# Attention scores of a hybrid decoder layer: hi and lo parts packed as two halves of 64 rows, and mask with row maximum in one vector instruction

## The chip, the core and the metric

The kernel runs on one core of one Trainium2 chip. The metric is the device time of one execution in microseconds (us). Several executions were timed; the median is used, and a profile was taken of one further execution.

## The reference

The layer takes 1024 tokens of width 1024 in float32. A normalised input is projected once, and the columns of that projection feed two mixers side by side: a Mamba-2 scan (SSD, 16 heads of 64) and differential attention (8 heads). Their outputs are joined, projected, and a gated feed-forward network (FFN) and a last norm follow. The change concerns the differential attention:

```python
q = q.reshape(bsz, seqlen, DA_HEADS, 2, DA_HEAD_DIM).transpose(3, 0, 2, 1, 4) * (DA_HEAD_DIM ** -0.5)
k = k.reshape(bsz, seqlen, DA_HEADS, 2, DA_HEAD_DIM).transpose(3, 0, 2, 1, 4)
...
        s = jnp.einsum("mbhqd,mbhkd->mbhqk", qi, k).astype(f32)
        qpos = i * Q_BLOCK + jnp.arange(Q_BLOCK)
        mask = kpos[None, :] <= qpos[:, None]
        p = jax.nn.softmax(jnp.where(mask, s, -jnp.inf), axis=-1)
        w = p[0] - lam * p[1]
        return jnp.einsum("bhqk,bhkv->bhqv", w.astype(v.dtype), v)
```

Every head has two maps (m = 0 and 1). Each map has its own 64 columns of q and k, its own causal softmax, and the difference of the two maps weights v. A block is 128 queries, so a head has 8 blocks, and block i sees (i + 1) x 128 keys.

## The kernel before

The work stands in the program in this order: the mixer norm; the SSD part in two groups; the attention, head by head; the output projection (lines 660 to 725); the FFN; the down projection. All arithmetic of the matmuls is of float32 accuracy: an operand is split into a rounded part "hi" (type `float32r`) and the exact rest "lo", and a product is taken as hi·hi + hi·lo + lo·hi. `mm3` (lines 126 to 129) is that product, three matmuls into one accumulator; the projections, the output projection and the FFN all use it.

The order on each engine is not written out by hand in the attention. The tile framework orders the instructions of the whole program by its own simulated time line, within the dependencies and with the pools as limits. So projections of the next heads stand between the attention matmuls of the present one. From line 909 on, TensorE's order is the written one.

One head of the attention runs through these functions.

- `v_pair` (line 527) projects v for two heads. `qk` (line 543) projects k and q for one head: `proj_T` gives 128 columns (64 of each map) by 512 tokens in a PSUM tile, for two halves of the tokens, and a sink takes it out of PSUM.
- `sink_k` (lines 547 to 553) writes a tile `KS` with one plane for each map: k-hi of the map on its own 64 rows and k-lo of the same map on the other 64 rows. That is one ScalarE copy and one VectorE subtraction of 64x512 for each map.
- `sink_q` (lines 555 to 566) writes `QH` and `QL`, again a plane for each map, with q-hi (or q-lo) on both halves of the rows. For each map that is a ScalarE multiplication (562), a VectorE instruction (563), and a copy to the other half on ScalarE (565) and on VectorE (566).
- `att_front` (lines 572 to 598) makes the scores of one block. With that packing, one matmul over all 128 rows gives q-hi·(k-hi + k-lo), a second gives q-lo·(k-hi + k-lo): lines 585 and 586, for each map and each chunk of at most 512 keys. Block i has one chunk for i below 4 and two from there on. Then VectorE adds the causal mask `cneg` to the 128 columns of the diagonal (587), takes the negated row maximum (588), and ScalarE takes the exponential with the row sum (590). Lines 593 to 597 join the two maps.
- `att_back` (line 600) transposes the weights (607), copies them out (608) and multiplies by v (611). `att_norm` and `att_out` follow later. `step` calls them one block or more behind the front.

Score tiles come from the pool `SC`, which has two buffers of 1024 columns (two banks of PSUM each). `KS`, `QH` and `QL` come from `A4`, 14 buffers of 1024 float32 columns; for the last head one tile of `QL` comes from `CV`. The exponentials are in `P4`. The output projection's first part (line 696, tiles `po_s`) needs the SSD output alone and runs beside the last heads; its loads of x and its stores of h are issued from GpSimd's queue (695 and 698), as are the loads of h (704).

Of the kernel before, what the change touches and what calls it, by code (L numbers as in the profile page):

```python
# [9 lines left out]
F32 = mybir.dt.float32  # L10
F32R = mybir.dt.float32r
AF = mybir.ActivationFunctionType
ALU = mybir.AluOpType
# [11 lines left out]
def tile_hybrid_block(  # L25
# [68 lines left out]
    def norm_rows(parts, wbc, outs, name, pool=(), junk=None):  # L94
        """outs = RMSNorm of the row whose column pieces are parts; pieces in pool are weighted on Pool and scaled on ACT"""
        n, w = len(parts), DM // len(parts)
        ss = small.tile([P, n], F32, tag="ss1", name="ss_" + name)
        for i, p in enumerate(parts):
            nc.scalar.activation(outs[i] if junk is None else junk, p, AF.Square, accum_out=ss[:, i:i + 1])
        if n > 1:  # L100
            s1 = small.tile([P, 1], F32, tag="ss1", name="st_" + name)
            nc.vector.tensor_tensor(s1, ss[:, 0:1], ss[:, 1:2], op=ALU.add)
            ss = s1
        r = rstd_of(ss, DM, name)
        for i, (p, o) in enumerate(zip(parts, outs)):
            wi = wbc[:, i * w:i * w + w]
            if i in pool:
                nc.gpsimd.tensor_tensor(o, p, wi, op=ALU.mult)
                nc.scalar.mul(o, o, r)
            else:  # L110
                nc.vector.scalar_tensor_tensor(o, p, r, wi, op0=ALU.mult, op1=ALU.mult)
# [34 lines left out]
    def A4(shape, dt, name):  # L146
        return a4.tile(shape, dt, tag="a4", name=name)
# [15 lines left out]

# [1 line left out]
    def load_raw(src, shape, name):  # L165
# [14 lines left out]
    def z0_raw(a, u):  # L180
        """columns of dt and of the gate of group 0: 264 of 528"""
        raw = wp.tile([P, 4, 264], F32, tag="raw", bufs=2, name=f"wr_z0_{a}_{u}")
        k = slice(4 * u, 4 * u + 4)
        if a == 0:
            nc.sync.dma_start(raw[:, :, 0:16], w_in_k[:, k, C_DT:C_DT + 16])
            nc.sync.dma_start(raw[:, :, 16:264], w_in_k[:, k, C_Z:C_Z + 248])
        else:
            nc.sync.dma_start(raw, w_in_k[:, k, C_Z + 248:C_Z + 512])
        return raw
# [6 lines left out]

# [1 line left out]
    xs = []  # L198
# [16 lines left out]

# [1 line left out]
    prow = P4([69, P], F32, "prow")  # L217
# [17 lines left out]

# [1 line left out]
    def w_unit(src, shape, name, alloc=None):  # L237
# [10 lines left out]
    def proj_T(*jobs):  # L248
        """each job: a weight, a column, a name and sink(half, psum [128 columns, 512 tokens])"""
        us = [w_unit(w_k[:, :, col:col + P], [P, KD, P], name) for w_k, col, name, _ in jobs]  # L250
# [7 lines left out]
    def proj_z0(us, name, sink):  # L258
        """units of 264 columns; sink(t, psum [128 tokens, 264])"""
        for t in range(NT):  # L260
# [8 lines left out]
    def proj_nat(col, name, sink):  # L269
        """256 columns; sink(t, psum [128 tokens, 2 blocks from t, 256])"""  # L270
        us = [w_unit(w_in_k[:, 4 * u:4 * u + 4, col:col + 256], [P, 4, 256], f"{name}_{u}") for u in range(2)]
# [9 lines left out]

# [1 line left out]
    W16 = [P, NT, 16]  # L283
# [49 lines left out]

# [1 line left out]
    def conv_tiles(*tiles):  # L335
# [21 lines left out]
    def gate_dt():  # L357
        """the gate of group 0 and dt"""
        for a in range(2):
# [151 lines left out]

# [1 line left out]
    cneg = sp.tile([P, P], F32, tag="cs", name="cneg")  # L513
    nc.vector.memset(cneg, 0.0)
    nc.gpsimd.affine_select(cneg, cneg, [[-1, P]], ALU.is_ge, NEG, base=0, channel_multiplier=1)
    lv = CV([P, 4, 64], F32, "lv")
# [10 lines left out]
    def v_pair(hh):  # L527
        # [head][block] views of the two heads; in the last pair but one, the heads' tiles are freed one by one
        by_head = hh == NH // 2 - 2
# [13 lines left out]
    def qk(h):  # L543
        KS, QH, QL = [], [], []
        own = (slice(0, 64), slice(64, 128))

        def sink_k(half, ps):
            ks = A4([P, 2, 512], F32R, f"KS{h}_{half}")
            KS.append(ks)
            for m in range(2):  # L550
                a, b = own[m], own[1 - m]
                nc.scalar.copy(ks[a, m, :], ps[a, :])
                nc.vector.tensor_tensor(ks[b, m, :], ps[a, :], ks[a, m, :].bitcast(F32), op=ALU.subtract)

        def sink_q(half, ps):
            qh = A4([P, 2, 512], F32R, f"QH{h}_{half}")
            ql = (CV if h == NH - 1 and half == 0 else A4)([P, 2, 512], F32R, f"QL{h}_{half}")
            QH.append(qh)
            QL.append(ql)
            for m in range(2):  # L560
                a, b = own[m], own[1 - m]
                nc.scalar.mul(qh[a, m, :], ps[a, :], 0.125)
                nc.vector.scalar_tensor_tensor(ql[a, m, :], ps[a, :], 0.125, qh[a, m, :].bitcast(F32),
                                               op0=ALU.mult, op1=ALU.subtract)
                nc.scalar.copy(qh[b, m, :], qh[a, m, :].bitcast(F32))
                nc.vector.tensor_copy(ql[b, m, :], ql[a, m, :].bitcast(F32))
        jobs = ((w_in_k, C_K + h * P, f"k{h}", sink_k), (w_in_k, C_Q + h * P, f"q{h}", sink_q))
        for js in ([jobs] if h == NH - 1 else [[j] for j in jobs]):
            proj_T(*js)
        return KS, QH, QL  # L570

    def att_front(h, i, KS, QH, QL):
        n = f"{h}_{i}"
        Lk = (i + 1) * P
        qs = slice(i * P, (i + 1) * P)
        pm = []
        nmx = small.tile([P, 2], F32, tag="nmx", name="nmx" + n)
        sm = small.tile([P, 2], F32, tag="sm", name="sm" + n)
        for m in range(2):
            s = SC([P, T], f"s{n}_{m}")  # L580
            qr = slice((i % 4) * P, (i % 4) * P + P)
            for c in range(i // 4 + 1):
                w = min(Lk - c * 512, 512)
                sc = s[:, c * 512:c * 512 + w]
                nc.tensor.matmul(sc, QH[i // 4][:, m, qr], KS[c][:, m, :w], start=True, stop=False)
                nc.tensor.matmul(sc, QL[i // 4][:, m, qr], KS[c][:, m, :w], start=False, stop=True)
            nc.vector.tensor_tensor(s[:, qs], s[:, qs], cneg, op=ALU.add)
            nc.vector.reduce_max(nmx[:, m:m + 1], s[:, :Lk], axis=AX.X, negate=True)  # L588
            p = P4([P, T], F32, f"p{n}_{m}")
            nc.scalar.activation(p[:, :Lk], s[:, :Lk], AF.Exp, bias=nmx[:, m:m + 1], accum_out=sm[:, m:m + 1])  # L590
            pm.append(p)
# [67 lines left out]

# [1 line left out]
    KG = 4  # L661
# [14 lines left out]
    def out_block(t, kys, ws, name, bank=MM):  # L676
        """two token blocks from t, 256 columns"""
        ps = bank([P, 2, 256], f"po_{name}_{t}")
# [47 lines left out]

# [1 line left out]
    # gate and up by Winograd's seven products: A are two column tiles by two halves of the contraction, B the two  # L728
    # halves of the contraction by two halves of the tokens; C = A B is summed up in PSUM (X, Y and Z)
    ORDER = (1, 2, 6, 5, 7, 3, 4)  # L730
# [4 lines left out]
    def room(p, early):  # L735
        """an operand B: [hi or lo][block of 128 rows] views of 512 tokens"""
        if early:
# [59 lines left out]
    def ffn_pair(pr, raws, order=ALL, ybank=SC):  # L797
        """silu(gate) * up of two column tiles; they and their sums as operands of the down projection to g_d"""
        sg, tm, c22, reg, sm = {}, {}, {}, [{}, {}], [{}, {}]
# [145 lines left out]
    def final_half(t, nh, last):  # L945
        """the first half of a row to be ready is weighted before its scale is known"""
        ho = h_parts(ho_all, t)
# [12 lines left out]

    # down, by the same seven products: A are the two halves of the tokens by two row tiles, B the row tiles by two
    # halves of the columns
    SLOT = {2: 0, 4: 1, 1: 2, 7: 3, 5: 4, 6: 5, 3: 6}
# [28 lines left out]
    for gi, prs in enumerate(groups):  # L992
# [5 lines left out]
        def psums(two, name):  # L998
            """four banks: one for each block of 128 tokens of a half"""
            if two:  # L1000
# [81 lines left out]
```

## Time and profile before

| | us |
|---|---|
| median of 3 runs | 1641.82 |
| lowest, highest | 1639.54, 1644.53 |
| span of the profiled execution | 1643.3 |

The profile is read as follows. "PE" is TensorE's matmuls and "PEld" its weight loads; DVE is VectorE, ACT ScalarE, POOL GpSimd. Busy time is the time in which at least one instruction of the engine is recorded. A matmul is recorded from its start to a modelled end, and the next one starts before that end; so the distance from one start to the next, its pitch, says how fast the stream runs, and the recorded duration does not. The shape `128*128 128x512` names the stationary operand and then the moving one, so 512 is the number of keys or tokens that one matmul streams. The attention's first score matmul starts at 387 us and its last at 848 us; projections of the heads start somewhat earlier, beside the SSD scan.

| stretch of the span, us | what runs in it | PE busy | DVE busy | ACT busy |
|---|---|---|---|---|
| 0 to 340 | norm, SSD | 320.11 | 187.39 | 184.62 |
| 340 to 860 | end of SSD, attention, first output projection | 514.13 | 378.03 | 304.46 |
| 860 to 1643 | output projection, FFN, down | 763.00 | 506.17 | 286.76 |

### The profile page before, as it was taken

To read this page: it belongs to the slowest core of one execution; us is meant where nothing else is said; L and a number is where in the kernel's file an instruction comes from. 1 tells how busy PE (TensorE), PEld (TensorE's weight loads), DVE (VectorE), ACT (ScalarE), POOL (GpSimd) and SP (SyncE) were. 2 spreads that over 40 slices of the span, in tenths; PEclk is the share of its full clock that TensorE was granted. 3 is DMA by queue.
4 is the path that set the end of the run, shared out by engine and by line. 5 is a ranking of instruction groups with operands and counts; after the bars stand their busy time and mean duration, and the time that the engine had idled before them with its cause. 6 is when DMAs were issued, how large, how long until landed. Compare 5 with 4: busy or idle time off the path is not lost. (4 is left out here: it accounts for less than half of the span.)

```text
span 1643.3 us, 23716 instructions
## 1 busy us (share of the span) xinstructions
PE 1597.2 (97%) x9170; PEld 1386.9 (84%) x9170; DVE 1071.6 (65%) x1682; ACT 775.8 (47%) x1608; POOL 429.2 (26%) x378
## 2 busy tenths in 40 slices
PE   6999999999999999999999998999999999999997
PEld 6988878887989989889999987888888888778885
DVE  5345745688776676677674477455555555898987
ACT  6444764456555565575552245333333333334445
POOL 4100330032000000013300034444444443542322
PEclk9999999999999999999999999999999999999999
DMA  5321451143011110147523221233333323944122
GB/s 195 110 79 52 129 163 56 36 142 92 24 46 39 46 33 27 45 130 229 162 77 116 84 99 56 96 102 104 111 116 118 98 96 134 365 166 186 39 103 103
DMA packets 105291, 172.78 MB, mean 105 GB/s; under 512 B 7813, under 2 KB 75530, under 8 KB 103770
## 3 DMA queue, kind: packets, MB, share of 16 engines
q1 hardware_dynamic: 95210, 137.11, 25.2%
q0 software_dynamic: 9968, 34.15, 6.3%
q8 instruction: 72, 1.18, 0.3%
q14 instruction: 41, 0.34, 0.1%
HBM read 125.82 MB, written 45.42 MB: 104 GB/s over the span
## 5 line engine op out<-in xcount | busy, mean ns | idle before, releaser
L127 PE MATMUL x<-n,wa 128*128 128x512 f32 x352 | 138.7, 396 | 0.0
L128 PE MATMUL x<-n,wa 128*128 128x512 f32 x352 | 138.7, 394 | 0.0
L129 PE MATMUL x<-n,wa 128*128 128x512 f32 x352 | 137.8, 394 | 0.0
L590 ACT ACTIVATE p<-s,nmx 128x256 f32<-128x256 f32 (+7 forms) x128 | 94.4, 740 | 53.2 <-DVE nmx L588 49.9
L172 ACT CAST wa<-s 128x512 fp32r<-128x512 f32 x88 | 54.7, 622 | 132.3 <-PE x L129 59.4
L173 DVE TENSOR_TENSOR wa<-s,wa 128x512 fp32r<-128x512 f32 x88 | 76.8, 873 | 51.1 <-ACT wa L172 50.8
L172 ACT CAST dg<-gd 128x512 fp32r<-128x512 f32 x77 | 47.7, 620 | 114.7 <-PE dx L129 57.2
L588 DVE TENSOR_REDUCE nmx<-s 128x1 f32<-128x256 f32 (+7 forms) x128 | 95.3, 754 | 2.4
L173 DVE TENSOR_TENSOR dg<-gd,dg 128x512 fp32r<-128x512 f32 x77 | 66.2, 862 | 23.3 <-ACT dg L172 23.2
L129 PEld LDWEIGHTS x<-n,wa 128*128 128x128 f32 x352 | 66.5, 189 | 15.1
L128 PEld LDWEIGHTS x<-n,wa 128*128 128x128 f32 x352 | 66.6, 189 | 14.8
L127 PEld LDWEIGHTS x<-n,wa 128*128 128x128 f32 x352 | 66.6, 189 | 14.8
L127 PE MATMUL mm_z<-wh_z,nhi 128*128 128x264 f32 (+1 forms) x256 | 75.9, 298 | 2.3 <-ACT wh_z L172 2.3
L611 PE MATMUL o<-v,p 128*128 128x128 f32 x576 | 77.7, 275 | 0.0
L129 PE MATMUL mm_z<-wh_z,nlo 128*128 128x264 f32 (+1 forms) x256 | 77.3, 303 | 0.0
L611 PEld LDWEIGHTS o<-v,p 128*128 128x128 f32 x576 | 73.5, 191 | 2.7
L128 PE MATMUL mm_z<-wl_z,nhi 128*128 128x264 f32 (+1 forms) x256 | 75.0, 294 | 0.0
L127 PE MATMUL mm_v<-wh_v,nhi 128*128 128x256 f32 x256 | 74.2, 290 | 0.0
L129 PE MATMUL mm_v<-wh_v,nlo 128*128 128x256 f32 x256 | 74.1, 290 | 0.0
L128 PE MATMUL mm_v<-wl_v,nhi 128*128 128x256 f32 x256 | 73.5, 287 | 0.0
L128 PE MATMUL po_a<-wl_wo,yh 128*128 128x256 f32 x256 | 72.6, 283 | 0.0
L91 POOL TENSOR_TENSOR rs_o<-ms_o,mhalf 128x4 f32<-128x4 f32 x16 | 18.0, 1125 | 208.4 <-DVE ms_o L89 208.3
(331 smaller groups left out, 5172.9 us busy)
## 6 DMA issues: line engine op xcount, KB each, us to landing
gd<-g_d SPq DMA_DIRECT2D x11, 1792.0 KB, 7.8
wr_g<-in_w_gate_dram SPq DMA_DIRECT2D x22, 512.0 KB, 3.8
wr_u<-in_w_up_dram SPq DMA_DIRECT2D x22, 512.0 KB, 4.3
g_d<-sg SPq DMA_DIRECT2D x22, 512.0 KB, 5.1
wr_d<-in_w_down_dram SPq DMA_DIRECT2D x22, 512.0 KB, 5.0
L<-cs_d POOLq DMA_DIRECT2D x16, 512.0 KB, 4.4
wr_y<-yT_d SPq DMA_DIRECT2D x16, 512.0 KB, 3.8
wr_wo<-in_w_out_dram SPq DMA_DIRECT2D x16, 512.0 KB, 3.5
```

The source lines that it names most:

```text
L91: nc.gpsimd.tensor_tensor(r, ms, mhalf[:, :w], op=ALU.pow)
L127: nc.tensor.matmul(ps, lh, rh, start=first, stop=False, skip_group_check=more)
L128: nc.tensor.matmul(ps, lh, rl, start=False, stop=False, skip_group_check=more)
L129: nc.tensor.matmul(ps, ll, rh, start=False, stop=last, skip_group_check=more)
L172: nc.scalar.copy(hi, raw)
L173: nc.vector.tensor_tensor(lo, raw, hi.bitcast(F32), op=ALU.subtract)
L588: nc.vector.reduce_max(nmx[:, m:m + 1], s[:, :Lk], axis=AX.X, negate=True)
L590: nc.scalar.activation(p[:, :Lk], s[:, :Lk], AF.Exp, bias=nmx[:, m:m + 1], accum_out=sm[:, m:m + 1])
L611: nc.tensor.matmul(o, wT[:, j * P:(j + 1) * P], vt[h % 2][j], start=(j == 0), stop=(j == i))
```

## The change

Three things are changed; docstrings and comments are removed besides, which are left out here.

1. `sink_k` and `sink_q` write one tile `KS` and one tile `QS` for each half of the tokens, with plane 0 = hi and plane 1 = lo over all 128 rows, as the projection gives them: map 0 is on rows 0 to 63 and map 1 on rows 64 to 127. Nothing is written to another half or twice.
2. The scores are three matmuls for each map, hi·hi, hi·lo and lo·hi, each over the map's own 64 rows. The two maps alternate, so both score tiles are taken from `SC` at the start of a block. The product lo·lo, which the earlier packing included, is not computed.
3. The mask becomes a tile of 128x1024 from `A4`, zero but for its last 128 columns. One `tensor_tensor_reduce` over all keys adds it, negates the sum in place in PSUM and returns the minimum, which is the negated row maximum. The exponential takes the scores with scale -1.

```diff
-    cneg = sp.tile([P, P], F32, tag="cs", name="cneg")
+    cneg = A4([P, T], F32, "cneg")
     nc.vector.memset(cneg, 0.0)
-    nc.gpsimd.affine_select(cneg, cneg, [[-1, P]], ALU.is_ge, NEG, base=0, channel_multiplier=1)
+    nc.gpsimd.affine_select(cneg[:, T - P:], cneg[:, T - P:], [[-1, P]], ALU.is_ge, NEG, base=0, channel_multiplier=1)
...
         def sink_k(half, ps):
             ks = A4([P, 2, 512], F32R, f"KS{h}_{half}")
             KS.append(ks)
-            for m in range(2):
-                a, b = own[m], own[1 - m]
-                nc.scalar.copy(ks[a, m, :], ps[a, :])
-                nc.vector.tensor_tensor(ks[b, m, :], ps[a, :], ks[a, m, :].bitcast(F32), op=ALU.subtract)
+            nc.scalar.copy(ks[:, 0, :], ps)
+            nc.vector.tensor_tensor(ks[:, 1, :], ps, ks[:, 0, :].bitcast(F32), op=ALU.subtract)
 
         def sink_q(half, ps):
-            qh = A4([P, 2, 512], F32R, f"QH{h}_{half}")
-            ql = (CV if h == NH - 1 and half == 0 else A4)([P, 2, 512], F32R, f"QL{h}_{half}")
...
-            for m in range(2):
-                a, b = own[m], own[1 - m]
-                nc.scalar.mul(qh[a, m, :], ps[a, :], 0.125)
-                nc.vector.scalar_tensor_tensor(ql[a, m, :], ps[a, :], 0.125, qh[a, m, :].bitcast(F32),
-                                               op0=ALU.mult, op1=ALU.subtract)
-                nc.scalar.copy(qh[b, m, :], qh[a, m, :].bitcast(F32))
-                nc.vector.tensor_copy(ql[b, m, :], ql[a, m, :].bitcast(F32))
+            qs = A4([P, 2, 512], F32R, f"QS{h}_{half}")
+            QS.append(qs)
+            nc.scalar.mul(qs[:, 0, :], ps, 0.125)
+            nc.vector.scalar_tensor_tensor(qs[:, 1, :], ps, 0.125, qs[:, 0, :].bitcast(F32),
+                                           op0=ALU.mult, op1=ALU.subtract)
...
-        for m in range(2):
-            s = SC([P, T], f"s{n}_{m}")
-            qr = slice((i % 4) * P, (i % 4) * P + P)
-            for c in range(i // 4 + 1):
-                w = min(Lk - c * 512, 512)
-                sc = s[:, c * 512:c * 512 + w]
-                nc.tensor.matmul(sc, QH[i // 4][:, m, qr], KS[c][:, m, :w], start=True, stop=False)
-                nc.tensor.matmul(sc, QL[i // 4][:, m, qr], KS[c][:, m, :w], start=False, stop=True)
-            nc.vector.tensor_tensor(s[:, qs], s[:, qs], cneg, op=ALU.add)
-            nc.vector.reduce_max(nmx[:, m:m + 1], s[:, :Lk], axis=AX.X, negate=True)
+        ss = [SC([P, T], f"s{n}_{m}") for m in range(2)]
+        for c in range(i // 4 + 1):
+            w = min(Lk - c * 512, 512)
+            for j, (a, b) in enumerate(((0, 0), (0, 1), (1, 0))):
+                for m in range(2):
+                    o = slice(64 * m, 64 * m + 64)
+                    nc.tensor.matmul(ss[m][:, c * 512:c * 512 + w], QS[i // 4][o, a, qr], KS[c][o, b, :w],
+                                     start=j == 0, stop=j == 2)
+        for m, s in enumerate(ss):
+            nc.vector.tensor_tensor_reduce(s[:, :Lk], s[:, :Lk], cneg[:, T - Lk:], op0=ALU.add, op1=ALU.min, scale=-1.0,
+                                           scalar=3.0e38, accum_out=nmx[:, m:m + 1])
             p = P4([P, T], F32, f"p{n}_{m}")
-            nc.scalar.activation(p[:, :Lk], s[:, :Lk], AF.Exp, bias=nmx[:, m:m + 1], accum_out=sm[:, m:m + 1])
+            nc.scalar.activation(p[:, :Lk], s[:, :Lk], AF.Exp, bias=nmx[:, m:m + 1], scale=-1.0,
+                                 accum_out=sm[:, m:m + 1])
```

More of the change, by code (lines that the diff above doesn't have):

```diff
@@ L543, in qk @@
     def qk(h):
-        KS, QH, QL = [], [], []
-        own = (slice(0, 64), slice(64, 128))
+        KS, QS = [], []
         def sink_k(half, ps):
@@ L549, in sink_k @@
             KS.append(ks)
-            for m in range(2):
-                a, b = own[m], own[1 - m]
-                nc.scalar.copy(ks[a, m, :], ps[a, :])
-                nc.vector.tensor_tensor(ks[b, m, :], ps[a, :], ks[a, m, :].bitcast(F32), op=ALU.subtract)
+            nc.scalar.copy(ks[:, 0, :], ps)
+            nc.vector.tensor_tensor(ks[:, 1, :], ps, ks[:, 0, :].bitcast(F32), op=ALU.subtract)
         def sink_q(half, ps):
-            qh = A4([P, 2, 512], F32R, f"QH{h}_{half}")
-            ql = (CV if h == NH - 1 and half == 0 else A4)([P, 2, 512], F32R, f"QL{h}_{half}")
-            QH.append(qh)
-            QL.append(ql)
-            for m in range(2):
-                a, b = own[m], own[1 - m]
-                nc.scalar.mul(qh[a, m, :], ps[a, :], 0.125)
-                nc.vector.scalar_tensor_tensor(ql[a, m, :], ps[a, :], 0.125, qh[a, m, :].bitcast(F32),
-                                               op0=ALU.mult, op1=ALU.subtract)
-                nc.scalar.copy(qh[b, m, :], qh[a, m, :].bitcast(F32))
-                nc.vector.tensor_copy(ql[b, m, :], ql[a, m, :].bitcast(F32))
+            qs = A4([P, 2, 512], F32R, f"QS{h}_{half}")
[3 more added lines that the diff above has]
+                                           op0=ALU.mult, op1=ALU.subtract)
         jobs = ((w_in_k, C_K + h * P, f"k{h}", sink_k), (w_in_k, C_Q + h * P, f"q{h}", sink_q))
@@ L569, in qk, with att_front @@
             proj_T(*js)
-        return KS, QH, QL
-    def att_front(h, i, KS, QH, QL):
+        return KS, QS
+    def att_front(h, i, KS, QS):
         n = f"{h}_{i}"
         Lk = (i + 1) * P
-        qs = slice(i * P, (i + 1) * P)
+        qr = slice((i % 4) * P, (i % 4) * P + P)
         pm = []
```

## The prediction

> **What bounds the kernel now.** I read the busy times first, then the stretches, then the source view of the score matmuls, and last the time line inside the attention.
>
> ```profile
> span 1643.3 us, 23716 instructions
> PE 1597.2 (97%) x9170; PEld 1386.9 (84%) x9170; DVE 1071.6 (65%) x1682; ACT 775.8 (47%) x1608; POOL 429.2 (26%) x378
> ...
> 340.00:860.00 520.00, 514.13 (x3408) 465.78 (x3407) 378.03 (x710) 304.46 (x748) 69.94 (x90) 1.00 0.27 83
> ...
> 340.00:395.00 55.00, 53.64 (x275) 42.79 (x274) 49.09 (x78) 32.62 (x78) 16.53 (x22) 1.00 0.40 121
> 420.00:700.00 280.00, 280.00 (x1790) 252.29 (x1789) 187.56 (x370) 159.26 (x396) 14.64 (x18) 1.00 0.13 38
> ```
>
> After each stretch come its length, then busy time and count of PE, PEld, DVE, ACT and POOL, the granted clock, the DMA share and GB/s. From 420 to 700 us PE is busy in all of the 280 us at a clock of 1.00, while DVE has 33% and ACT 43% to spare. Over the whole attention stretch PE is idle for 520 - 514.13 = 5.87 us. So the stage is bound by the number and pitch of TensorE's instructions: what is taken from that stream shortens the kernel one for one, as long as the other engines keep up. Only at the start, beside the SSD scan (340 to 395 us), is DVE the fullest after PE, at 49.09 of 55 us.
>
> ```profile
> L585 PE MATMUL s<-KS,QH x192: 219/389/504, 387.3 to 847.5; 128*128 128x512 f32 x96, 128*128 128x128 f32 x32, 128*128 128x256 f32 x32, 128*128 128x384 f32 x32
> L586 PE MATMUL s<-KS,QL x192: 272/387/482, 387.3 to 847.7; 128*128 128x512 f32 x96, 128*128 128x128 f32 x32, 128*128 128x256 f32 x32, 128*128 128x384 f32 x32
> ```
>
> There are 384 score matmuls. Their pitch is read from starts, not from durations:
>
> ```profile
> 599.77 0.39 PE L585 MATMUL s<-KS,QH 128*128 128x512 f32 x1
> 600.00 0.39 PE L586 MATMUL s<-KS,QL 128*128 128x512 f32 x1
> 600.22 0.28 PE L585 MATMUL s<-KS,QH 128*128 128x256 f32 x1
> 600.34 0.29 PE L586 MATMUL s<-KS,QL 128*128 128x256 f32 x1
> 600.46 0.40 PE L129 MATMUL mm_q<-nhi,wl_q 128*128 128x512 f32 x1
> ...
> 609.86 0.34 PE L585 MATMUL s<-KS,QH 128*128 128x384 f32 x1
> 610.04 0.34 PE L586 MATMUL s<-KS,QL 128*128 128x384 f32 x1
> 610.21 0.40 PE L127 MATMUL mm_q<-nhi,wh_q 128*128 128x512 f32 x1
> ...
> 503.63 0.19 PEld L585 LDWEIGHTS s<-KS,QH 128*128 128x128 f32 x1
> 503.69 0.27 PE L585 MATMUL s<-KS,QH 128*128 128x128 f32 x1
> 503.74 0.19 PEld L586 LDWEIGHTS s<-KS,QL 128*128 128x128 f32 x1
> 503.80 0.28 PE L586 MATMUL s<-KS,QL 128*128 128x128 f32 x1
> ```
>
> 512 keys take 0.23 us (599.77 to 600.00), 384 take 0.175, 256 take 0.12. At 128 keys two matmuls stand 0.11 apart, exactly as far as their weight loads (503.63 and 503.74): there the load sets the pace. By the counts above a map of a head has 6, 2, 2 and 2 chunks of these widths, in one matmul each way, which makes 6 x 0.23 + 2 x (0.175 + 0.12 + 0.11) = 2.19 us. With two matmuls, two maps and eight heads that is 32 x 2.19 = **70.1 us** of the stream.
>
> **The change part by part.**
>
> *Scores.* Six matmuls for a chunk instead of four, each on half of the rows. No row shows a matmul on 64 rows, nor two at once, so the cost is bounded. If the two maps' halves run side by side, three pairs take the place of four: 52.6 us, a saving of 17.5. If each half takes a slot of its own: 1.5 x 70.1 = 105.2 us, a loss of 35. Between them, if halves run side by side but loads stay one at a time at 0.11 us, a pair can't be shorter than 0.22: 24 x (6 x 0.23 + 6 x 0.22) = 64.8 us, a saving of 5.3. I take side by side, since the two maps' matmuls share no row, no operand and no PSUM bank, and for the loads the middle of 17.5 and 5.3: **-11.4 us**.
>
> The Trainium skill ("TensorE: Matmul & The Clock Gate", Part 3) says that tiles on different row groups run at the same time and gives 3.07 times for four 32-row tiles. No run here shows it. By that figure two halves would come out near the first bound.
>
> *Turning between full and half rows.* In the time line of before the 384 matmuls stand in 125 unbroken runs, with projections, transposes or products with v between them. After the change the two maps of a chunk go together, so there are between 64 runs (one per block) and 125; I take 95, so 190 turns. The nearest thing in the trace is a transpose let into the stream:
>
> ```profile
> 396.48 0.39 PE L127 MATMUL mm_q<-nhi,wh_q 128*128 128x512 f32 x1
> 396.71 0.27 PE L607 MATMUL wtp<-ident,p 128*128 128x128 f32 x1
> 396.74 0.48 PE L128 MATMUL mm_q<-nlo,wh_q 128*128 128x512 f32 x1
> 397.06 0.40 PE L129 MATMUL mm_q<-nhi,wl_q 128*128 128x512 f32 x1
> ...
> L586 PE MATMUL s<-KS,QL 128*128 128x512 f32 x96 | 38.1, 397 | 0.0
> ```
>
> From 396.71 to 397.06 the two take 0.35, against 0.11 + 0.23 by themselves: 0.01 for the turn, or **+1.9 us** for 190. The upper end is a full emptying of the pipe, the recorded 0.397 less the pitch of 0.23, or 0.167 each: 31.7 us. The lower end is nothing.
>
> *Leaving PSUM.* Per head and half of the tokens, k and q go out in one ACT and one DVE instruction each, instead of two (with two copies more of q).
>
> ```profile
> L552 ACT CAST KS<-mm_k x32: 563/580/583, 348.0 to 715.6; 64x512 fp32r<-64x512 f32 x32
> L553 DVE TENSOR_TENSOR KS<-mm_k,KS x32: 683/689/694, 349.6 to 716.6; 64x512 fp32r<-64x512 f32 x32
> L562 ACT ACTIVATE QH<-mm_q x32: 572/592/597, 366.6 to 744.8; 64x512 fp32r<-64x512 f32 x32
> L563 DVE SCALAR_TENSOR_TENSOR QL<-mm_q,QH x32: 662/689/696, 370.7 to 747.5; 64x512 fp32r<-64x512 f32 x32
> L565 ACT CAST QH<-QH x32: 616/618/621, 367.8 to 747.4; 64x512 fp32r<-64x512 f32 x32
> L566 DVE CAST QL<-QL x32: 420/422/559, 372.6 to 749.1; 64x512 fp32r<-64x512 f32 x32
> L124 DVE TENSOR_TENSOR nlo<-pt_n,nhi 128x512 fp32r<-128x512 f32 x16 | 10.8, 687 | 12.9 <-ACT nhi L123 12.9
> ```
>
> A subtraction of 128x512 (L124, 687 ns) takes as long as one of 64x512 (689). So ACT goes from 32 x (0.580 + 0.592 + 0.618) = 57.3 to 16 x 1.172 = 18.8 us, and DVE from 32 x (0.689 + 0.689 + 0.422) = 57.6 to 16 x 1.378 = 22.0.
>
> *Mask and maximum.*
>
> ```profile
> L587 DVE TENSOR_TENSOR s<-s,cneg 128x128 f32<-128x128 f32 x128 | 36.8, 294 | 31.4 <-PE s L586 30.2
> L588 DVE TENSOR_REDUCE nmx<-s 128x1 f32<-128x512 f32 x16 | 10.8, 689 | 0.4
> L590 ACT ACTIVATION_READ_ACCUMULATOR p<-s,nmx 128x1 f32 x128 | 25.2, 197 | 0.0
> L1008 DVE TENSOR_TENSOR h<-dx,h 128x512 f32<-128x512 f32 x64 | 40.0, 679 | 1.5 <-PE dx L129 1.4
> ```
>
> The fused instruction is not in this trace. Adding PSUM and SBUF over 512 columns (L1008, 679 ns) costs what the maximum costs (689), so I price it like the maximum alone: DVE loses the 36.8 us of line 587. If its result is read out by a second instruction, as ACT's row sum is (197 ns), 25.2 of that comes back. Together DVE loses 47 to 72 us and ACT 38.5 us, nearly all of it beside a full PE, so it is worth nothing there. It counts where PE waits: 5.87 us at most. I take **-2 us**, since 1.36 of the idle time falls where DVE is nearly full (340 to 395) and most of the rest has other causes. What is late next is the PE stream itself. The once-only filling of the wider mask and the room in `A4` (1 + 4 tiles beside the last head, against 5) cost nothing measurable.
>
> *A new wait.* Both score tiles are now taken before the first matmul of a block, so it waits for the second exponential of the block before, where it waited for the first.
>
> ```profile
> 486.00 0.39 PE L585 MATMUL s<-KS,QH 128*128 128x512 f32 x1
> ...
> 487.01 1.01 ACT L590 ACTIVATE p<-s,nmx 128x896 f32<-128x896 f32 x1 [2.15 <-DVE nmx L588]
> ...
> its engine sat idle before it (us, times) until:
>   ACT p L590: 6.4, 6
> ```
>
> The last line is what the score matmuls wait for that exponential now. Here block 7 of a head starts 2.0 us before that exponential ends. The same comparison over the 63 changes of block gives 17 such cases with 22.9 us in all. Queued behind the waiting matmul on PE would be projections of the next head, transposes and products with v, and ACT and DVE would wait for those. I take 0: such a block has only to stand later in a stream that holds, per head, 96 projection matmuls of 0.23 us for k and q alone. Bounds: 0 to +22.9.
>
> *Sum:* -11.4 + 1.9 - 2.0 = -11.5 us, against a profiled span of 1643.3, which lies 1.5 above the median of the runs and inside their spread; taken from the median, 1641.8 - 11.5 = **1630.3 us**.
>
> **The rivals.**
>
> *Loads one at a time.* For it: 0.11 us between loads at 128 keys. Against: they would go to different rows. -5.3 + 1.9 - 2.0 = -5.4: 1636.4.
>
> *Each turn empties the pipe: slower.* At 0.167 us each turn, 190 turns cost 31.7: -11.4 - 2.0 + 31.7 = +18.3, 1660. It decides from 13.4/190 = 0.07 us a turn. For it: the interleaving that keeps PE full makes the turns. Against: the transpose's 0.01. The Trainium skill ("TensorEngine Tiling (Array Packing)", Tiling Modes, Key Properties) states this rule, "Mode switching requires drain", with no figure; no run here shows it.
>
> *The halves don't run side by side,* so the change doesn't do what it says: +35.1 + 1.9 - 2.0 = +35.0, 1677. For it: no row shows two matmuls at once. Against: nothing in the trace but their separate rows.
>
> *The new wait is exposed in full:* -11.5 + 22.9 = +11.4, 1653.
>
> **How the numbers follow.** About 0.3% (4.9 us) is what a measurement of this kernel tells from no change. Forecast 0.50, 0.04 of it within 0.3%; loads one at a time 0.12, half within and half faster; emptying 0.17, 0.05 of it within (where a turn costs about 0.07) and 0.12 slower; no overlap 0.17; exposed wait 0.04. Faster 0.46 + 0.06 = 0.52; the same 0.04 + 0.06 + 0.05 = 0.15; slower 0.12 + 0.17 + 0.04 = 0.33. The forecast's own range is 1618 (-17.5 and the whole 5.9 of idle time) to 1637. The range asked for goes up to the emptying, 1662, and leaves out the case without overlap.
>
> **What would show it.** The starts of the two maps' matmuls, row by row: almost equal, or 0.23 apart at 512 keys. The distance of pairs at 128 and 256 keys: 0.12, or 0.22 and more. The first projection matmul behind a run of scores, and the first score behind a projection: later than the pitch, or not. Idle time of PE put down to the exponential of line 590: 6.4 us in the source view of before, or some 20. DVE's and ACT's busy time between 340 and 860: lower by 47 to 72 and by some 38. The forecast is wrong if the score stream takes over 70 us, or if the schedule lets PE go idle where it was full.

## The result and the profile after

The changed kernel takes 1713.66 us (median of 4 runs, 1713.42 to 1714.87) against 1642.34 before. The ratio is 1.0432, with a 95% interval from 1.0413 to 1.0451: 71 us slower. A time of 1630.3 was forecast, and 1662 was the upper end of the range. (The title's words on hi and lo parts in two halves of 64 rows fit the kernel before; in the changed kernel the two halves of the rows hold the two maps, and hi and lo are two planes over all rows.)

From the page of the changed kernel, then the same two stretches of its time line as before (length, then PE, PEld, DVE, ACT, POOL):

```profile
span 1711.4 us, 23983 instructions
PE 1673.5 (98%) x9362; PEld 1410.9 (82%) x9362; DVE 1011.6 (59%) x1618; ACT 739.6 (43%) x1544; POOL 429.0 (25%) x378
...
340.00:930.00 590.00, 589.80 (x3606) 489.37 (x3605) 316.01 (x646) 269.75 (x688) 71.36 (x92) 1.00 0.23 75
420.00:700.00 280.00, 280.00 (x1665) 228.16 (x1664) 136.11 (x302) 123.32 (x326) 14.05 (x17) 1.00 0.10 31
```

Up to 340 us PE is busy for 320.96 us (320.11 before), and the part behind the attention lasts 781 us (783 before); the attention stretch has grown by 70 us. PE is still busy in all of it, at a clock of 1.00, while DVE has gone from 187.56 to 136.11 us between 420 and 700, and ACT from 159.26 to 123.32. So the other engines don't hold TensorE up. TensorE's own stream is longer, and yet it runs fewer matmuls in the same 280 us (1665 against 1790), with fewer loads.

The groups of the new lines (578 are the score matmuls, 581 the fused instruction):

```profile
L578 PE MATMUL s<-KS,QS 64*128 64x512 f32 x288 | 85.7, 426 | 0.0
L578 PEld LDWEIGHTS s<-KS,QS 64*128 64x128 f32 x576 | 82.6, 185 | 34.3 <-issue 12.5 <-ACT p L603 2.3 <-ACT p L609 0.4
L581 DVE CUSTOM_DVE_ANT_0 s<-s,cneg 128x1024 f32<-128x1024 f32 x16 | 19.7, 1232 | 22.0 <-PE s L578 22.0
L581 DVE DVE_READ_ACCUMULATOR2_ANT nmx<- 128x1 f32 x128 | 18.1, 142 | 0.0
```

The tile is now `64*128`: the matmuls do run on half of the rows. The fused instruction costs what the maximum cost (1232 ns at 1024 columns), with a read-out of 142 ns. A weight load of 64 rows takes 185 ns, as one of 128 rows did (188). New is 12.5 us of idle time before the scores' loads that is put down to "issue": the engine waited for nothing that the profile shows.

How the maps follow each other is seen in the order of TensorE's instructions in the built program, TensorE's queue. Here is block 4 of head 0 (row, line, output<-inputs, shape; like instructions in succession share a row, and the head's number is left out of the names; `s_4_0` is map 0, `s_4_1` map 1):

```
1873 L578 MATMUL s_4_0_3548<-KS_0_3340,QS_1_3430 128x512 x3
1874 L578 MATMUL s_4_0_3548<-KS_1_3368,QS_1_3430 128x128 x3
1875 L128 MATMUL mm_v_0_4219<-wl_v_0_4210,nhi_134 128x256
...
1883 L606 MATMUL o_2_3540<-v_0_3095,p_2_1_3498 128x128 x3
1884 L578 MATMUL s_4_1_3549<-KS_0_3340,QS_1_3430 128x512 x3
1885 L578 MATMUL s_4_1_3549<-KS_1_3368,QS_1_3430 128x128 x3
```

The program alternates the maps; the schedule does not. All matmuls of map 0 come first, then projections and products with v, then map 1. The 576 score matmuls stand in 139 unbroken runs, and only 57 times in all does one map follow the other inside a run. Between the runs stand matmuls on full rows, and in the records no score matmul starts ahead of one of those. So the halves can meet only in the 17 runs that hold both maps.

Inside such a run they need not be neighbours. In block 1 of head 3 the queue has three matmuls of map 0 and then three of map 1, each over 256 keys. Three views of this run, taken over ever longer stretches, and what follows it (start, time from the first start to the last end, count):

```profile
581.28 0.39 PE L578 MATMUL s<-KS,QS 64*128 64x256 f32 x2
...
581.28 0.51 PE L578 MATMUL s<-KS,QS 64*128 64x256 f32 x4
...
581.28 0.63 PE L578 MATMUL s<-KS,QS 64*128 64x256 f32 x6
581.84 0.39 PE L129 MATMUL mm_v<-wh_v,nlo 128*128 128x256 f32 x1
```

They start in twos, 10 to 14 ns apart, and each further two add 0.12 us, the pitch of one matmul at 256 keys: the first of map 1 started ahead of the second and third of map 0, which stand before it in the queue. In five blocks where six of map 0 precede six of map 1 the records show the same, by their widths. Even so, only 48 of the 288 possible pairs start together in the changed kernel.

What a run costs is read in the time line of the changed kernel, matmuls and loads, at two blocks of 128 keys:

```profile
513.29 0.47 PE L129 MATMUL mm_k<-nhi,wl_k 128*128 128x512 f32 x1
513.70 0.55 PE L578 MATMUL s<-KS,QS 64*128 64x128 f32 x3
514.17 0.50 PE L127 MATMUL mm_k<-nhi,wh_k 128*128 128x512 f32 x1
514.51 0.39 PE L128 MATMUL mm_k<-nlo,wh_k 128*128 128x512 f32 x1
514.83 0.55 PE L578 MATMUL s<-KS,QS 64*128 64x128 f32 x3
515.30 0.50 PE L129 MATMUL mm_k<-nhi,wl_k 128*128 128x512 f32 x1
515.64 0.39 PE L127 MATMUL mm_k<-nhi,wh_k 128*128 128x512 f32 x1
515.86 0.40 PE L128 MATMUL mm_k<-nlo,wh_k 128*128 128x512 f32 x1
...
514.17 0.19 PEld L127 LDWEIGHTS mm_k<-nhi,wh_k 128*128 128x128 f32 x1
514.83 0.41 PEld L578 LDWEIGHTS s<-KS,QS 64*128 64x128 f32 x3 [0.36 <-issue]
515.30 0.19 PEld L129 LDWEIGHTS mm_k<-nhi,wl_k 128*128 128x128 f32 x1
515.64 0.19 PEld L128 LDWEIGHTS mm_k<-nlo,wh_k 128*128 128x128 f32 x1
```

A projection matmul of 512 followed by another takes 0.22 to 0.23 us (515.64 to 515.86). With a score behind it, it takes 0.32 (514.51 to 514.83); the first one behind a run takes 0.34 (515.30 to 515.64). The loads say why the second of these is long: the load for the matmul at 515.86 begins at 515.64, one matmul ahead, but the loads of the matmuls at 514.83 and 515.30 begin only with these matmuls. At a turn the load is not taken ahead: in all 139 runs the load of the first score starts within 5 ns of its matmul, on full rows (`e2_full_rows`, below) in 2 of 139.

Over all 139 runs of the changed kernel, against the same rows of kernel `e2_full_rows` below, which has the same order without turns, the medians are (pitch in us):

| place | full rows | half rows | difference |
|---|---|---|---|
| last projection matmul before a run, 512 wide | 0.232 | 0.33 | 0.09 to 0.10 |
| last transpose or product with v before a run | 0.03 | 0.20 | 0.17 |
| first score of a run at 512, if not one of a pair | 0.23 | 0.337 | 0.105 |
| last score of a run at 512 | 0.231 | 0.324 | 0.09 |
| first 512-wide projection matmul behind a run | 0.235 | 0.337 | 0.10 |

So a run on half rows, with a turn at either end, costs 0.39 us behind a projection and 0.47 behind a transpose or a product with v: about **0.2 us for each turn**.

### The profile page after: what moved, and what is told of

It is laid out like the page before. It is cut to its first block, busy times and chain, and to the rows that moved or that the text cites. A ratio compares the mean times of both kernels' runs of the same rounds, so it can differ in the third digit from the quotient of the medians.

```text
span 1711.4 us, 23983 instructions
## 1 busy us (share of the span) xinstructions
PE 1673.5 (98%) x9362; PEld 1410.9 (82%) x9362; DVE 1011.6 (59%) x1618; ACT 739.6 (43%) x1544; POOL 429.0 (25%) x378
## 5 line engine op out<-in xcount | busy, mean ns | idle before, releaser
L581 DVE CUSTOM_DVE_ANT_0 s<-s,cneg 128x256 f32<-128x256 f32 (+7 forms) x128 | 97.0, 769 | 113.2 <-PE s L578 113.0
L578 PE MATMUL s<-KS,QS 64*128 64x512 f32 (+3 forms) x576 | 131.6, 368 | 0.0
L578 PEld LDWEIGHTS s<-KS,QS 64*128 64x128 f32 x576 | 82.6, 185 | 34.3 <-issue 12.5
```

The costliest lines, as they stand in the source:

```text
L578: nc.tensor.matmul(ss[m][:, c * 512:c * 512 + w], QS[i // 4][o, a, qr], KS[c][o, b, :w], start=j == 0, stop=j == 2)
L581: nc.vector.tensor_tensor_reduce(s[:, :Lk], s[:, :Lk], cneg[:, T - Lk:], op0=ALU.add, op1=ALU.min, scale=-1.0, scalar=3.0e38, accum_out=nm ...
```

## The experiments

Each ratio below is to runs of the kernel before that were made in the same session. Two theories stand against each other on why the stream grew. In the first, which the order suggests, the halves would run side by side if the schedule let them, and the loss is the slots of the 192 added matmuls (a slot is the stretch of the stream that one matmul takes) and the turns. In the second the halves never run side by side. A third puts part of the loss down to the fused instruction.

**Pairs held together** (`e1_paired`).

```diff
+        with tc.manual_schedule(engines={mybir.EngineType.PE, mybir.EngineType.DVE}):
+            for s in ss:
+                nc.vector.memset(s[:, 0:1], 0.0)
...
-                for m in range(2):
+                for m in (1, 0):
```

> The changed kernel, but with the two maps' score matmuls held together on TensorE: the six matmuls of a chunk stand in an order that the scheduler may not change, map 1 first, and a one-column memset on VectorE ties map 1's first matmul to both score tiles. The score matmuls then stand in 73 runs, with the maps in turn. Theory A (halves run side by side once they are neighbours, the schedule had taken them apart, each turn between full and half rows costs about 0.1 us): three pair slots, 52.6 us instead of before's 70.1, plus 73 runs x 2 turns x 0.1 = 15 us, less some 2 us for the lighter evictions: about 1637 to 1643, level with before. Rival B (the halves don't run side by side): only 66 runs fewer, about 1698. Rival C (side by side, but weight loads one at a time at 0.11 us): 64.8 + 15 - 70.1 = +10, about 1652.

Measured: 1662.56 us, 1.0114 of before [1.0097, 1.0131]. The maps alternate in the order, in 73 runs. Three views of the same run of six matmuls 512 wide, taken over ever longer stretches, then what follows it (start, time from the first start to the last end, count):

```profile
600.75 0.48 PE L127 MATMUL mm_q<-nhi,wh_q 128*128 128x512 f32 x1
601.16 0.50 PE L581 MATMUL s<-KS,QS 64*128 64x512 f32 x2
...
601.16 0.73 PE L581 MATMUL s<-KS,QS 64*128 64x512 f32 x4
...
601.16 0.96 PE L581 MATMUL s<-KS,QS 64*128 64x512 f32 x6
602.05 0.50 PE L128 MATMUL mm_q<-nlo,wh_q 128*128 128x512 f32 x1
602.39 0.40 PE L129 MATMUL mm_q<-nhi,wl_q 128*128 128x512 f32 x1
```

Each pair adds 0.23 us, which is the time of a single matmul before: the halves run fully side by side. In the records the second of a pair mostly starts 3 to 10 ns after the first. At 128 keys pairs stand 0.06 and 0.11 us apart, as single matmuls on full rows do, so the loads of the two halves go side by side too. That settles rivals B and C: neither holds. The Trainium skill ("TensorE: Matmul & The Clock Gate", Part 3) says that tiles on different row groups run at the same time, a few nanoseconds apart; this trace agrees, with a median of 3 ns at 512 columns and a factor of 2.

The time is nevertheless 20 us above what theory A gave at its upper end. With the two sizes of the table, 53 runs behind projections and 20 behind transposes or products with v cost 53 x 0.39 + 20 x 0.47 = 30 us and not 15; my expectation had counted the 0.09 on each side and not the loads. Against before that makes -17.5 + 30 - 3.8 (the lighter evictions, below) = +9; +18.7 was measured. Most of the rest is idle time of PE:

```profile
sum 550.00, PE 538.66 PEld 467.83 DVE 321.95 ACT 269.47 POOL 68.88; mean PE 76.95 PEld 66.83 DVE 45.99 ACT 38.50 POOL 9.84
...
PE s L581 <- DVE s L575: 3.3, 3, 2.1
PE po_a L127 <- DVE hx L695: 2.9, 1, 2.9
```

These are the sum of the stretches from 340 to 890 us and the longest waits of PE from 340 to 900: 11.3 us idle, against 4.0 in the same stretch of `e5_two_full`. Of this, 3.3 us are behind the memset that waits for both score tiles (L575); whether the tie brought the rest is not shown.

**The same order on full rows** (`e2_full_rows`). The scores are sums over both maps.

```diff
-                    o = slice(64 * m, 64 * m + 64)
-                    nc.tensor.matmul(ss[m][:, c * 512:c * 512 + w], QS[i // 4][o, a, qr], KS[c][o, b, :w],
+                    nc.tensor.matmul(ss[m][:, c * 512:c * 512 + w], QS[i // 4][:, a, qr], KS[c][:, b, :w],
```

> The changed kernel with the same order of TensorE's instructions, but each of the 576 score matmuls runs over all 128 rows, so that the scores are sums over both maps and not the reference's. There is no turn between full and half rows. Theory A: the turns go, 139 runs x (0.09 going in, up to 0.17 behind a transpose, and 0.09 coming out) = 25 to 30 us, so about 1683 to 1688, and what stays against before is the 192 added slots. Rival (half-row matmuls are slow in themselves, whatever stands beside them): less than 10 us below the changed kernel's 1713 if the rows don't matter, or far more than 30 if they do.

Measured: 1674.00 us, 1.0182 [1.0165, 1.0198]. The order of TensorE's instructions has the same 139 runs. So half rows cost 39.7 us and not the 25 to 30 expected, again because each turn also shows a load. From the table: 93 runs behind projections and 46 others make 93 x 0.39 + 46 x 0.47 = 58 us; the 48 pairs that do run side by side give some 14 back (the pitches inside runs sum to 84.2 us against 83.5 here, although about 139 x 0.105 = 14.6 of the turns is in the 84.2); 44 are left. Of the 4 us between this and the 39.7, 1.8 is idle time of PE, 2.0 us here from 340 to 890 us against 0.2 in the changed kernel. Half-row matmuls aren't slow in themselves: inside a run, two of one map at 512 keys stand 0.23 us apart, as on full rows.

**The fused instruction alone, in the kernel before** (`e3_fused_only`).

```diff
-            nc.vector.tensor_tensor(s[:, qs], s[:, qs], cneg, op=ALU.add)
-            nc.vector.reduce_max(nmx[:, m:m + 1], s[:, :Lk], axis=AX.X, negate=True)
+            nc.vector.tensor_tensor_reduce(s[:, :Lk], s[:, :Lk], cneg[:, T - Lk:], op0=ALU.add, op1=ALU.min, scale=-1.0,
+                                           scalar=3.0e38, accum_out=nmx[:, m:m + 1])
...
```

The wider mask tile and the exponential's scale of -1 come with it.

> The kernel before with the fused mask and maximum alone (scores packed as before). Theory A: VectorE's saving lies beside a full TensorE, so no change: 1640 to 1644. Rival (the fused instruction, which writes the whole score tile back to PSUM and is read out by a second instruction, holds up the exponentials): over 1655.

Measured: 1646.03 us, 1.0012 [1.0001, 1.0023], with before at 1644.49 in the same session. That is 2 us over the upper end of what was expected and far from the rival's 1655: the fused instruction is no gain, and costs 0.2% at most.

**The changed kernel without the fused instruction** (`e4_no_fused`): the exchange above the other way round, mask tile and scale included.

> The changed kernel with the separate mask and maximum of before; packing, three products and half rows stay, and the scheduler is free (136 runs, the maps mostly apart). Theory A (the loss is all in TensorE's order): no change against the changed kernel's 1713.7, so 1706 to 1720. Rival (the fused instruction has a part in the loss, by delaying the release of the score tiles, which sets how the maps are placed): below 1700.

Measured: 1708.17 us, 1.0397 [1.0383, 1.0412]. The loss stays. The 5 us less go with another schedule (136 runs, with 82 meetings of the maps in place of 57); that this is their cause is argued, not shown.

**Two products on full rows** (`e5_two_full`): as `e2_full_rows`, and in the loop over products

```diff
-            for j, (a, b) in enumerate(((0, 0), (0, 1), (1, 0))):
+            for j, (a, b) in enumerate(((0, 0), (0, 1))):
...
```

> The changed kernel with all 128 rows in each score matmul and only two products for each map (hi-hi and hi-lo; lo-hi is left out), so the scores are not the reference's. TensorE then has as many score matmuls, of the same widths, as the kernel before, and no turns; the lighter evictions and the fused mask stay. Theory A: these are worth what the prediction took for them, about 2 us: 1636 to 1642. Rival (VectorE and ScalarE had held TensorE up through the attention more than the idle time shows): below 1630.

Measured: 1639.81 us, 0.9977 [0.9966, 0.9989]. This has the kernel before's count of score matmuls and no turns, so 0.23%, or 3.8 us (1.8 to 5.6 by the interval), is what the lighter evictions and the fused mask are worth together, if the small difference in the order (129 runs for 125) is worth nothing. And `e2_full_rows` less this one, 1674.0 - 1639.8 = 34.2 us, is the price of 192 further slots; the prediction's bound for it was 35.

**Fewer runs** (`e6_merged`): the paired kernel, with the scores of two blocks in one run while both fit.

```diff
+        with tc.high_priority(), tc.manual_schedule(engines={mybir.EngineType.PE, mybir.EngineType.DVE}):
...
+            for z, i in enumerate(blocks):
...
+                            nc.tensor.matmul(ss[m][:, c + z, :w], QS[i // 4][o, a, qr], KS[c][o, b, :w],
+                                             start=j == 0, stop=j == 2)
...
+        if i > 3 or i % 2 == 0:
+            scores(h, [i] if i > 3 else [i, i + 1], KS, QS)
```

> The paired kernel with fewer runs: the scores of blocks 0 and 1 and of blocks 2 and 3 are made together (each fits in half a score tile), and the score matmuls have the scheduler's first priority, so that they stand in 48 unbroken runs of six pairs, against 73. Theory A (what keeps the paired kernel 18 us above before is the turns, about 0.4 us for a run: 0.09 and 0.1 going in, as much coming out): 25 runs fewer give 10 us, so about 1652, and down to 1640 if the waits that the tie added go too. Rival (it is the waiting for both score tiles, not the turns): a run holds both tiles for two blocks, so nothing is won: 1660 or more.

Measured: 1654.65 us, 1.0066 [1.0052, 1.0079]. Against the paired kernel that is 7.9 us less for 25 runs fewer, 0.32 each; theory A had 10, the rival none. Idle time of PE went the other way:

```profile
sum 550.00, PE 536.59 PEld 472.28 DVE 320.10 ACT 269.56 POOL 71.36; mean PE 76.66 PEld 67.47 DVE 45.73 ACT 38.51 POOL 10.19
...
720.00:800.00 80.00, 72.52 (x594) 67.91 (x593) 50.52 (x116) 38.98 (x97) 26.71 (x36) 0.96 0.60 194
```

From 340 to 890 us it is 13.4 us, 7.5 of it between 720 and 800, where the clock granted fell to 0.96. With 37 x 0.39 + 11 x 0.47 = 19.6 us of turns, an estimate of -17.5 + 19.6 - 3.8 = -1.7 us would be left against before without the added idle time, so even well scheduled this packing would come out about level here. That was not tried.

**The kernel before, with its copies of q on GpSimd** (`e7_pool_copies`).

```diff
-                nc.scalar.copy(qh[b, m, :], qh[a, m, :].bitcast(F32))
-                nc.vector.tensor_copy(ql[b, m, :], ql[a, m, :].bitcast(F32))
+                nc.gpsimd.tensor_copy(qh[b, m, :], qh[a, m, :].bitcast(F32))
+                nc.gpsimd.tensor_copy(ql[b, m, :], ql[a, m, :].bitcast(F32))
```

> The kernel before, with its two copies of q to the other half of the rows moved from ScalarE (line 565) and VectorE (line 566) to GpSimd, which is idle there for most of the time. It takes 19.8 us off ScalarE and 13.7 us off VectorE and leaves TensorE's stream as it is. Theory A (lighter evictions are worth a little: the two-product kernel, with 38 us less on ScalarE and some 50 less on VectorE, came out at 0.998 of before): 0.998 to 1.000, about 1639 to 1643. Rival (q comes later, since GpSimd is slower, and TensorE waits for it): over 1646.

Measured: 1641.40 us against 1644.48 in the same session, 0.9983 [0.9972, 0.9995]. The stretch from 340 to 860 us has ACT at 288.26 in place of 304.46 and POOL at 119.88 in place of 69.94:

```profile
340.00:860.00 520.00, 516.41 (x3428) 468.00 (x3427) 366.32 (x679) 288.26 (x717) 119.88 (x154) 1.00 0.27 83
```

It falls where theory A had it, and it is the only version that computes the reference and comes out ahead of both kernels, by a small margin.

## Why the prediction was wrong

The forecast is put together again with what the runs measured:

| term | predicted, us | measured, us |
|---|---|---|
| scores: six matmuls on half rows for four | -11.4 | +34.2, as slots (`e2_full_rows` less `e5_two_full`) |
| turns | +1.9 | +39.7, with what the few overlaps win already taken off (after less `e2_full_rows`) |
| evictions, mask, maximum | -2.0 | -3.8 (`e5_two_full` against before) |
| new wait for both score tiles | 0 | none in the changed kernel; with pairs held together 3.3 at the tie, up to 7 of idle time in all |

The measured terms sum to 70.1; the change cost 71. They are differences along one chain of kernels, so that they add up proves nothing; what bears them out is the bound of 35 for the slots, and for the turns the pitches, which gave 44 against 39.7. (The 17 cases under the bound of 22.9 for the new wait come to 22.4 us in the records; the change didn't reach that wait.)

- *What bounds the kernel* was right: TensorE's stream alone, one for one. DVE and ACT were relieved by the forecast amounts (between 340 and 870 us DVE 382.0 before and 316.8 in `e5_two_full`, ACT 306.9 and 270.0), and it was worth about 4 us.
- *The step that failed first* is "I take side by side, since the two maps' matmuls share no row, no operand and no PSUM bank". That is true of the chip: pairs go at the pace of single matmuls, loads included, better than the middle that I took. But I carried the program's alternation over to TensorE's queue. The order there is the scheduler's, and it let map 0 go ahead, with matmuls on full rows behind it, so that 48 of 288 pairs ran together. Why the scheduler did so stays open. Both maps' tiles come from the pool of two, and the first comes free earlier (by 1.2 us in the median of the changed kernel's blocks), which would separate them; but the paired kernel fixed the order as well as adding the tie, so it doesn't single out the pool. On the chip the second tile was already free when map 0's first score started in 55 of the 63 changes of block of the changed kernel, so the separation is one of the schedule and not of a wait. The place was in the prediction under "a new wait": I asked what it costs if map 0 waits for both tiles, and not what happens if it doesn't wait. The listed outcome of 1677, "the halves don't run side by side", has the size of the slots right and the reason wrong.
- *The step that failed second* is the price of a turn. Between 0 and 0.167 us I took 0.01, from a transpose within the stream. A transpose keeps the tile at 128 rows, so it was no example of the thing. The rows show about 0.2 us for each turn, over my upper end: 0.09 to 0.17 before the turn's first matmul starts, where I had 0.167 at most for a full emptying, and 0.10 for a load that is not taken ahead, which I hadn't in the bound. With 139 runs in place of 95 the term is 58 us, before the overlaps. The rival "each turn empties the pipe" was right in that turns decide, and too low in price. The measured 0.2 us lies well over its point of decision of 0.07, and the paired kernel, with all of the overlap, is still slower than before.
- The Trainium skill ("TensorEngine Tiling (Array Packing)", Tiling Modes) states that changing the tiling mode drains the engine. The trace agrees, as far as it shows a wait of 0.09 to 0.17 us ahead of the first matmul of the turn; the ends of matmuls are modelled, so whether the pipe is empty then is not seen.
- *The fused instruction* went as priced: it costs what the maximum alone costs, and the time moves by 0.1%.

## What to carry to other kernels

Work on half of the rows pays only in long runs: here a run had to win back about 0.4 us, while a block's pairs win at most 0.46 us (two slots of 0.23, at 1024 keys) and 0.11 at 128 keys. Over the eight blocks of a head that is 17.5 / 8 = 2.2 us won against 8 x 0.39 = 3.1 paid, so it doesn't pay where one block makes one run between matmuls on full rows. Matmuls that are meant to run side by side must stand in one run with no matmul on full rows between them, and where a scheduler orders the queue, look at its order before counting on the overlap. In a stage where one engine is full, count its slots and what stands between them; 100 us taken off the other two engines were worth about 4 here.

## What was not expected of the hardware

- Two matmuls of 64 rows in different halves run at the full pace of one: starts 3 to 10 ns apart, pairs 0.23 us apart at 512 columns, and at 128 columns 0.06 and 0.11 us, so loads overlap as well.
- In a run on half rows, matmuls of one half can start ahead of matmuls of the other half that stand before them in the queue (three places in block 1 of head 3, in pairs 10 to 14 ns apart). In the kernels whose scores run on full rows or alternate strictly, all score and projection matmuls start in the queue's order.
- A turn between 128 and 64 rows costs about 0.2 us on either side of a run, half of it for a weight load that is not taken ahead (the load at 515.30 starts with its matmul, the one at 515.64 a matmul ahead).
- A `tensor_tensor_reduce` from and to PSUM takes 1232 ns at 1024 columns, as long as a maximum alone (1223 in the kernel before), and 142 ns more for reading out its result.
